# Halves of the first x tiles on two DMA queues, their scaling on three engines, and written orders at three places of a hybrid decoder block

## The chip, the cores and the metric

The kernel runs on one core of a Trainium2 chip. A core has five engines that run side by side, each with its own queue of instructions in order: TensorE (PE in the profile; PEld are its weight loads), VectorE (DVE), ScalarE (ACT), GpSimd (POOL) and SyncE (SP), which here only issues DMAs. ScalarE and GpSimd can issue DMAs too. Matrix products are written to PSUM, which has banks of 128 x 512 float32; all other tiles lie in SBUF. The metric is the device time of one execution in microseconds (us).

## The reference

The input x is 512 x 1024 float32. The block computes

```python
h = rmsnorm(x, norm1_g)
z = h @ w_in + b_in                      # split in five: glu, rx, rg, ga, gb
u = silu(layernorm(causal_conv31(glu(z_glu))))
y_a = u @ conv_w_out + conv_b_out
y_b = (rg_lru(causal_conv4(z_rx)) * gelu(z_rg)) @ lru_w_out
x = x + (sigmoid(z_ga) * y_a + sigmoid(z_gb) * y_b) @ w_mix_out
h = rmsnorm(x, norm2_g)
x = x + (silu(h @ w1) * (h @ w3)) @ w2
out = rmsnorm(x, norm_f_g)
```

where rmsnorm multiplies each row by the reciprocal root of its mean square and by a gain per column. For what follows three places matter: the first rmsnorm and the first columns of `h @ w_in`; the addition of the mixing product to x; and the last rmsnorm with the stores of the output.

## The kernel before, in words

Rows of x are taken in four tiles of 128 (t = 0 to 3), each in two halves of 512 columns: `xt[t][0]` and `xt[t][1]`. Every matrix product of float32 accuracy is made of three products of parts: each operand is split into a high part h (a copy to the type float32r) and a low part l (operand minus h), and h·h, h·l and l·h are accumulated (`mm3`, line 554). A weight chunk of 1024 columns a partition is loaded to a `raw` tile (`load_chunk`, 152), then its h is copied and its l subtracted (`emit_chunk`, 161). For the first chunk this is `first_parts` (128): VectorE copies the first 512 columns, GpSimd the second 512, and GpSimd subtracts both halves.

The start is as follows. SP issues the loads of x tiles 0 and 1, one DMA each (`load_x`, 508), two loads of parameter rows (`load_rows`, 499), the first weight chunk and the rest. ScalarE loads its table, warms a root (518) and makes a tile of ones (525). PE multiplies ones in the meantime (530). For each tile, half the sum of squares is made by VectorE in one reduction (`half_sum`, 640), the other half by ScalarE, then the root (`root`, 645 and 646) and VectorE's reciprocal. VectorE scales the halves in place (`scale_half`, 653). PE transposes the scaled rows 128 x 128 (`turn_rows`, 619) and the parameter rows (`rows_turned`, 542). ScalarE then writes the high parts of h (628), VectorE the low parts (629), and PE multiplies with the first chunk (673), in an order in which the products that need late parts come late.

The order of work on an engine comes from two sources. Most of the program is ordered by a planner, which takes the instructions in the order of the program as ranks and plays them through with estimated costs. Inside `tc.manual_schedule(engines=...)` the named engines keep the order as written. Before the change the first such region (684) names PE, ScalarE, VectorE and SP, so GpSimd is ordered by the planner there.

The mixing product and the last product are done in a scheme with seven products of quarters in place of eight (`Sevenfold.run`, 1173). At the end of its first group, products r1 and r2 of two row blocks i = 0, 1 lie in four PSUM banks, and VectorE adds each to x (`plus`, 1180). The mixing product alone is made with `behind=True`: what is split next for later products waits in VectorE's queue behind the last of these additions. The banks of r1 are accumulated into further by the second group, the banks of r2 become free for new products. After the second group VectorE makes five more additions, and the third group (`third`, 1215) accumulates into the banks of r1 again.

The last output tile is finished by `finish_last` (1587): add the last product in two halves of 256 columns, square and sum (ScalarE 1596, VectorE 1597), root and reciprocal (1598, 1600), scale with gain and reciprocal (1599, 1601, 1602, 1604), and store in three DMAs (SP 1603 and 1605, ScalarE 1606).

The core of the written order at the start:

```python
        r0 = first_sums(0)
        vec.reciprocal(r0, r0)
        scale_half(0, 0, r0)
        r1 = first_sums(1)
        scale_half(0, 1, r0)
        turn_rows(0, turned)
        vec.reciprocal(r1, r1)
        scale_half(1, 0, r1)
        rows_turned(0, n_first)
        scale_half(1, 1, r1)
        emit_to(1)
        turn_rows(1, turned)
```

Of the kernel before, what the change touches and what calls it, by code (L numbers as in the profile page):

```python
# [85 lines left out]
def tile_block(ctx, tc, a, out):  # L86
# [41 lines left out]
    def first_parts(h, l, full):  # L128
        vec.tensor_copy(h[:, :T], full[:, :T])
        pool_e.tensor_copy(h[:, T:], full[:, T:])  # L130
# [21 lines left out]
    def load_chunk(i):  # L152
        key, src, kt, cols = chunks[i][:4]
        raw = raws.tile([P, 1024], F32, tag="raw", name=f"raw_{key}")
        if callable(src):
# [343 lines left out]
    def load_rows(i):  # L499
        lo, m, src = parts[i]  # L500
        b, r = row_at(lo)
        nc.sync.dma_start(rowt[b][r : r + m, :P], src)
# [5 lines left out]
    def load_x(t):  # L508
        if t < PIECES:
# [4 lines left out]

    eps_t = consts.tile([P, 1], F32, name="eps_t")
# [15 lines left out]

    first = [i for i, (lo, _, _) in enumerate(parts) if lo < n_first]
    load_x(0)
    load_x(1)
    for i in first:
        load_rows(i)
# [77 lines left out]
    def turn_rows(t, ps):  # L614

        for c in (range(ND), (0, 3, 1, 2, 4, 7, 5, 6))[len(ps) == 6]:
# [35 lines left out]
    def scale_half(t, h, r):  # L652
        vec.tensor_scalar(out=xt[t][h], in0=xt[t][h], scalar1=r, scalar2=None, op0=ALU.mult)
# [30 lines left out]
    with tc.manual_schedule(engines={ET.PE, ET.Activation, ET.DVE, ET.SP}):  # L684
# [10 lines left out]
        rows_turned(0, n_first)  # L695
        scale_half(1, 1, r1)
# [433 lines left out]
    class Sevenfold:  # L1130
# [42 lines left out]
        def run(self, sums, begun, end):  # L1173
# [16 lines left out]
            for k in range(kh):  # L1190
# [396 lines left out]
    def finish_last(t, rest, plus_to):  # L1587
# [5 lines left out]
        for cs in HALVES:  # L1593
            plus_to(cs)
        x_ = x2[t][0]
        act.activation(junk[1][:, LO], x_[:, LO], AF.Square, accum_out=ss[:, 1:2])
        vec.tensor_tensor_reduce(out=o[0][:, HI], in0=x_[:, HI], in1=x_[:, HI], scale=1.0 / D, scalar=ss[:, 0:1], op0=ALU.mult, op1=ALU.add, accum_out=r)
        act.activation(r, ss[:, 1:2], AF.Sqrt, scale=1.0 / D, bias=r)
        vec.tensor_tensor(out=o[0][:, LO], in0=x_[:, LO], in1=gf[0][:, LO], op=ALU.mult)
        vec.reciprocal(r, r)  # L1600
        act.activation(o[1], o[1], AF.Copy, scale=r)
        vec.tensor_scalar(out=o[0][:, LO], in0=o[0][:, LO], scalar1=r, scalar2=None, op0=ALU.mult)
# [63 lines left out]
```

## Time and profile before

| what | value |
|---|---|
| median of 3 runs | 789.91 us (789.61 to 791.22) |
| profiled execution, its own time | 789.9 us |
| its span, first to last instruction | 788.1 us |
| TensorE busy | 779.7 us, 99% |
| VectorE, ScalarE, GpSimd busy | 679.0, 472.5, 363.6 us |
| moved by DMA | 199.04 MB, mean 253 GB/s |
| mean granted TensorE clock | 0.998 |

The span begins at 0; all times of rows count from there. A row of a timeline reads: start, duration, engine, line of the kernel, operation, output <- inputs, shapes, how many (x2: two merged into one row, the duration then runs from the start of the first to the end of the last). In brackets stands how long the engine had been idle and what ended that. An engine name with q (SPq, ACTq) is its sequencer, here one that issues a DMA: the duration is that of the issue, not of the transfer. Buffer numbers are left out of tile names.

### The profile page before, as it was taken

The numbers are of one execution on the slowest core, as the hardware profiler recorded it, in microseconds if no ns is written. First come the engines' busy times: TensorE is split into PE (matmuls) and PEld (weight loads), VectorE is DVE, ScalarE is ACT, GpSimd is POOL, SyncE is SP. The second block draws the span as 40 slices with busy tenths as digits, with TensorE's granted clock in tenths as the row PEclk, the third lists the DMA queues.
The fourth block names the chain that finished last, engine by engine and source line by source line (L and its number), as shares of the span: only waits on it lengthen the run. The fifth ranks groups of instructions, "written<-read, shape, count | busy, mean of one in ns | idle before, by whom it ended". The sixth has DMA issues, their size and how long they took to land.

```text
span 788.1 us, 12480 instructions
## 1 busy us (share of the span) xinstructions
PE 779.7 (99%) x4322; PEld 680.1 (86%) x4322; DVE 679.0 (86%) x1064; ACT 472.5 (60%) x693; POOL 363.6 (46%) x353
## 2 busy tenths in 40 slices
PE   9999999999999999999999999999999999999996
PEld 8988888888888888888887898999999999888885
DVE  6389998888989996999799969888777798999957
ACT  7544678966685966564325666555555555556843
POOL 3367777788779899545650591122222222000000
PEclk9999999999999999999999999999999999999999
DMA  7565989899889979999977896678998898779652
GB/s 226 144 192 156 271 237 264 246 260 296 256 239 297 269 213 272 294 284 304 321 270 250 253 287 200 200 243 306 334 307 282 297 309 302 239 238 266 204 169 107
DMA packets 191972, 199.04 MB, mean 253 GB/s; under 512 B 15245, under 2 KB 154149, under 8 KB 191909
## 3 DMA queue, kind: packets, MB, share of 16 engines
q1 hardware_dynamic: 182805, 166.52, 70.5%
q0 software_dynamic: 8960, 31.46, 11.7%
q8 instruction: 34, 0.56, 0.3%
q14 instruction: 29, 0.24, 0.1%
q10 hardware_dynamic: 144, 0.26, 0.1%
HBM read 146.30 MB, written 38.80 MB: 235 GB/s over the span
## 4 chain that ended last, share of the span: by engine, by line
PE 85%; DVE 8%; DMA 3%; issue 2%; ACT 1%; DVEq 0%; SPq 0%; ACTq 0%
PE z L563 36%; PE fr L1400 24%; PE or L1171 13%; PE f L563 3%; PE yb L563 3%; PE mxr L1171 3%; DMA raw_co<-in_conv_w_out_dram 2%; PE g L997 2%; PE fr L1444 1%; DVE hl_mxb L118 1%; DVE hl_co L118 1%; DMA raw_lo<-in_lru_w_out_dram 1%; DVE sga L1238 1%; DVE u L844 1%; PE th L603 1%
## 5 line engine op out<-in xcount | busy, mean ns | idle before, releaser
L797 DVE SCALAR_TENSOR_TENSOR cv<-u,par,cv 128x507 f32<-128x507 f32 (+15 forms) x240 | 162.6, 734 | 1.8 <-ACT cv L793 0.9
L118 POOL TENSOR_TENSOR hl_in<-raw_in,hl_in 128x1024 fp32r<-128x1024 f32 (+1 forms) x52 | 124.2, 2400 | 41.2 <-ACT hl_in L122 34.8
L118 POOL TENSOR_TENSOR fws<-fws 128x256 f32<-128x256 f32 x120 | 98.8, 825 | 80.3 <-DMA fws<-in_ffn_w_dram 74.3
L403 POOL DMA_DIRECT2D ot<-fwso x21 | 15.4, 733 | 164.1 <-DVE fwso L118 154.3
L1400 PE MATMUL fr<-hs_0h,hl_ft 128*128 128x256 f32 x320 | 59.2, 283 | 0.0
L122 ACT CAST hl_in<-raw_in 128x1024 fp32r<-128x1024 f32 x50 | 51.7, 1047 | 4.9 <-DMA raw_in<-in_w_in_dram 4.9
L118 DVE TENSOR_TENSOR hl_ft<-raw_ft,hl_ft 128x1024 fp32r<-128x1024 f32 x39 | 47.6, 1220 | 5.2 <-ACT hl_ft L122 5.2
L1400 PEld LDWEIGHTS fr<-hs_0h,hl_ft 128*128 128x128 f32 x320 | 50.6, 192 | 0.0
L122 ACT CAST hl_ft<-raw_ft 128x1024 fp32r<-128x1024 f32 x40 | 41.7, 1047 | 12.0 <-PE fr L1400 7.4
L118 DVE TENSOR_TENSOR hl_fb<-raw_fb,hl_fb 128x1024 fp32r<-128x1024 f32 x29 | 35.7, 1231 | 11.5 <-ACT hl_fb L122 11.5
L1400 PE MATMUL fr<-hs_0l,hl_ft 128*128 128x256 f32 x160 | 45.3, 283 | 0.0
L122 ACT CAST hl_fb<-raw_fb 128x1024 fp32r<-128x1024 f32 x30 | 31.5, 1049 | 18.2 <-PE fr L1400 12.2
L563 PE MATMUL z<-h10h,hl_in 128*128 128x512 f32 (+1 forms) x108 | 41.1, 382 | 0.0
L563 PE MATMUL z<-h12h,hl_in 128*128 128x512 f32 (+1 forms) x108 | 40.8, 379 | 0.0
L563 PE MATMUL z<-h14h,hl_in 128*128 128x512 f32 (+1 forms) x108 | 40.8, 379 | 0.0
L563 PE MATMUL z<-h15h,hl_in 128*128 128x512 f32 (+1 forms) x108 | 40.8, 379 | 0.0
L563 PE MATMUL z<-h16h,hl_in 128*128 128x512 f32 (+1 forms) x108 | 40.8, 379 | 0.0
L563 PE MATMUL z<-h13h,hl_in 128*128 128x512 f32 (+1 forms) x108 | 40.8, 379 | 0.0
L563 PE MATMUL z<-h11h,hl_in 128*128 128x512 f32 (+1 forms) x108 | 40.8, 379 | 0.0
L563 PE MATMUL z<-h17h,hl_in 128*128 128x512 f32 (+1 forms) x108 | 40.8, 379 | 0.0
L122 ACT CAST hl_ob<-raw_ob 128x1024 fp32r<-128x1024 f32 (+1 forms) x23 | 23.4, 1016 | 23.0 <-PE or L1171 12.3
L397 POOL TENSOR_TENSOR fws<-fws 128x256 f32<-128x256 f32 x40 | 32.5, 814 | 3.0
(930 smaller groups left out, 2596.9 us busy)
## 6 DMA issues: line engine op xcount, KB each, us to landing
raw_in<-in_w_in_dram SPq DMA_DIRECT2D x52, 512.0 KB
fws<-in_ffn_w_dram SPq DMA_DIRECT2D x40, 512.0 KB
raw_ft<-fs SPq DMA_DIRECT2D x34, 512.0 KB
fs<-fws SPq DMA_DIRECT2D x21, 512.0 KB
ot<-fwso POOLq DMA_DIRECT2D x21, 512.0 KB, 6.2
fwso<-in_ffn_w_dram POOLq DMA_DIRECT2D x40, 256.0 KB, 7.2
fs<-fws POOLq DMA_DIRECT2D x19, 512.0 KB, 4.6
raw_ob<-in_ffn_w_dram SPq DMA_DIRECT2D x33, 256.0 KB
```

What stands on the lines that cost most here:

```text
L118: return eng.tensor_tensor(out=o, in0=x, in1=y, op=ALU.subtract)
L122: copy(h, full)
L397: eng.tensor_tensor(out=q11, in0=q22, in1=q11, op=ALU.add)
L403: return queue.dma_start(dest, raw.rearrange("p (m n) -> p m n", n=256))
L563: pe.matmul(ps, l, r, start=i == 0, stop=i == n - 1)
L603: pe.transpose(ps[:, t * P : (t + 1) * P], src, ident)
L797: vec.scalar_tensor_tensor(out=acc[:, s:], in0=u[c][:, : T - s], scalar=dw(c, s), in1=acc[:, s:], op0=ALU.mult, op1=ALU.add)
L844: vec.tensor_tensor(out=u[c], in0=u[c], in1=rs, op=ALU.mult)
L997: pe.matmul(ps[:HB], head_chunk[0][:ROWS_G, g, h % 2, m, :], ext[h][m][:ROWS_G], start=m == 0, stop=m == 1)
L1171: pe.matmul(banks[i][:, cs], l_[:, ts], r_[:, cs], start=start and n == 0, stop=stop and n == 2, skip_group_check=again)
L1238: vec.scalar_tensor_tensor(out=o, in0=ps, scalar=pc("conv_b_out", j), in1=o, op0=ALU.add, op1=ALU.mult)
L1400: pe.matmul(ps[:, HALVES[i]], lw[:, c, :], rx_, start=not (again or i or c or m), stop=bool(i and c == 3 and m == 2), skip_group_check=True,)
```

## The change

- At the start the halves of x tiles 0 and 1 are loaded by two DMAs each, the first half from SP's queue and the second from ScalarE's; the two first loads of parameter rows go to ScalarE's queue as well. These loads are now issued ahead of ScalarE's table load.
- The first weight chunk is loaded in two DMAs of four blocks of rows each, that is of 512 columns of the raw tile. In `first_parts` GpSimd copies the first half, VectorE the second.
- x is scaled on three engines: the second half of tile 0 on GpSimd, the second half of tile 1 on ScalarE, the first halves on VectorE. The sums of tile 1 and the transposes of the parameter rows are written ahead of the scaling of tile 0's first half. Tile 0's second half is transposed first. GpSimd's order is as written in this region too.
- In the mixing product the four additions come in the order r1 of both row blocks, then r2 of both, behind all four products.
- In `finish_last` everything from the last additions on is in written order (ScalarE, VectorE, SP); ScalarE's last scaling is in two halves; the output's last tile goes out in four DMAs of 256 columns, three from SP and one from ScalarE.

```diff
     def first_parts(h, l, full):
-        vec.tensor_copy(h[:, :T], full[:, :T])
-        pool_e.tensor_copy(h[:, T:], full[:, T:])
+        pool_e.tensor_copy(h[:, :T], full[:, :T])
+        vec.tensor_copy(h[:, T:], full[:, T:])
         for cs in (slice(0, T), slice(T, 2 * T)):
             newest["sub"] = sub(pool_e, l[:, cs], full[:, cs], h[:, cs].bitcast(F32)).ins
...
-        if callable(src):
+        if i == 0:
+            for k in range(0, kt, 4):
+                nc.sync.dma_start(raw[:, k * cols : (k + 4) * cols].rearrange("p (k n) -> p k n", k=4), src[:, k : k + 4, :])
+        elif callable(src):
...
     def load_x(t):
+        if t < 2:
+            for h, queue in enumerate((nc.sync, nc.scalar)):
+                queue.dma_start(xt[t][h], x_nat[:, t, h * T : (h + 1) * T])
+            return
...
+    first = [i for i, (lo, _, _) in enumerate(parts) if lo < n_first]
+    load_x(0)
+    load_x(1)
+    for i in first:
+        load_rows(i, nc.scalar)
     eps_t = consts.tile([P, 1], F32, name="eps_t")
...
+        some = (0, 3, 1, 2, 4, 7, 5, 6)
+        for c in (range(ND), some[4:] + some[:4] if t == 0 else some)[len(ps) == 6]:
...
-    with tc.manual_schedule(engines={ET.PE, ET.Activation, ET.DVE, ET.SP}):
+    with tc.manual_schedule(engines={ET.PE, ET.Activation, ET.DVE, ET.SP, ET.Pool}):
...
         r0 = first_sums(0)
         vec.reciprocal(r0, r0)
+        scale_half(0, 1, r0, pool_e)
+        r1 = first_sums(1)
+        rows_turned(0, n_first)
         scale_half(0, 0, r0)
-        r1 = first_sums(1)
-        scale_half(0, 1, r0)
         turn_rows(0, turned)
         vec.reciprocal(r1, r1)
         scale_half(1, 0, r1)
-        rows_turned(0, n_first)
-        scale_half(1, 1, r1)
+        scale_half(1, 1, r1, act)
...
-                    if ends and r == 1:
+                    if ends and r == 1 and not self.behind:
                         plus(i, 0, r1[i])
-                        last_sum = plus(i, 0, r2[i]).ins
+                        plus(i, 0, r2[i])
+                    if ends and (r, i) == (1, 1) and self.behind:
+                        for b_ in (r1, r2):
+                            for t in range(2):
+                                last_sum = plus(t, 0, b_[t]).ins
...
+        with tc.manual_schedule(engines={ET.Activation, ET.DVE, ET.SP}):
+            for cs in HALVES:
+                plus_to(cs)
...
+            for cs in HALVES:
+                act.activation(o[1][:, cs], o[1][:, cs], AF.Copy, scale=r)
+            vec.tensor_scalar(out=o[0][:, LO], in0=o[0][:, LO], scalar1=r, scalar2=None, op0=ALU.mult)
+            vec.scalar_tensor_tensor(out=o[0][:, HI], in0=x_[:, HI], scalar=r, in1=gf[0][:, HI], op0=ALU.mult, op1=ALU.mult)
+            for queue, i, cs in ((nc.sync, 0, LO), (nc.sync, 1, LO), (nc.scalar, 1, HI), (nc.sync, 0, HI)):
+                queue.dma_start(o_nat[:, t, i * T + cs.start : i * T + cs.stop], o[i][:, cs])
```

More of the change, by code (lines that the diff above doesn't have):

```diff
@@ L530, in tile_block @@
         pe.matmul(wp[:, :P], ones, ones, start=True, stop=True)
[L532 to L536, printed above, removed]
     def rows_turned(c0, c1):
@@ L650, in first_sums, with scale_half @@
         return root(t, half_sum(t))
-    def scale_half(t, h, r):
-        vec.tensor_scalar(out=xt[t][h], in0=xt[t][h], scalar1=r, scalar2=None, op0=ALU.mult)
+    def scale_half(t, h, r, eng=vec):
+        if eng is act:
+            act.activation(xt[t][h], xt[t][h], AF.Copy, scale=r)
+        else:
+            eng.tensor_scalar(out=xt[t][h], in0=xt[t][h], scalar1=r, scalar2=None, op0=ALU.mult)
     HALVES = [slice(0, 256), slice(256, 512)]
```

23 lines of the change are left out of this document (7 added, 16 removed).

## The prediction

> **What bounds the kernel now.** First I read the busy table of the page, then the stages by window.
>
> ```profile
> PE 779.7 (99%) x4322; PEld 680.1 (86%) x4322; DVE 679.0 (86%) x1064; ACT 472.5 (60%) x693; POOL 363.6 (46%) x353
> ```
>
> ```profile
> 350.00:400.00 50.00, 50.00 (x222) 41.40 (x221) 43.27 (x56) 19.11 (x26) 27.07 (x28) 1.00 1.02 320
> 400.00:441.00 41.00, 40.63 (x179) 33.25 (x178) 40.26 (x61) 21.05 (x31) 5.85 (x8) 1.00 0.81 257
> ```
>
> TensorE (columns: length, then busy time of PE, PEld, DVE, ACT, POOL, then clock and DMA) is busy nearly without a break. So an edit can win time only where PE waits: at the start, before the first weights and inputs are ready; once near 428.9 us; and in the tail, after the last matmul. The change touches exactly these three. The second row also says that VectorE is busy for 40.26 of 41 us around the middle place, which decides the second term. The profiled execution took 789.9 us (span 788.1), the median of the runs 789.91, so no correction is needed.
>
> **Start: the present path.** Three views of the first 10 us, by engine: VectorE, ScalarE, TensorE.
>
> ```profile
> 5.78 0.49 DVE L653 TENSOR_SCALAR x<-x,stats 128x512 f32<-128x512 f32 x1
> 6.18 0.68 DVE L640 CUSTOM_DVE_ANT_0 n1j<-x 128x512 f32<-128x512 f32 x1
> ...
> 7.49 0.88 DVE L653 TENSOR_SCALAR x<-x,stats 128x512 f32<-128x512 f32 x2
> 8.29 0.42 DVE L129 CAST hl_in<-raw_in 128x512 fp32r<-128x512 f32 x1
> 9.16 0.48 DVE L629 SCALAR_TENSOR_TENSOR h10l<-tx,par,h10h 128x256 fp32r<-128x256 f32 x1 [0.45 <-ACT h10h L628]
> ```
>
> ```profile
> 0.73 1.28 ACT L518 ACT_TABLE_LOAD   x1 [0.73 <-PEq L1652]
> 2.03 0.20 ACT L518 ACTIVATE warm<-eps_t 128x1 f32<-128x1 f32 x1
> 2.14 0.28 ACT L525 CAST onesr<-ones 128x128 fp32r<-128x128 f32 x1
> 4.45 0.63 ACT L645 ACTIVATE n1j<-x 128x512 f32<-128x512 f32 x1 [2.03 <-DMA x<-in_x_dram]
> ...
> 5.75 0.63 ACT L645 ACTIVATE n1j<-x 128x512 f32<-128x512 f32 x1 [0.20 <-DMA x<-in_x_dram]
> ```
>
> ```profile
> 7.92 0.27 PE L542 MATMUL par_ps<-ident,rows 60*128 60x60 f32 x1
> 8.12 1.09 PE L619 MATMUL tx<-ident,x 128*128 128x128 f32 x8
> ```
>
> Tile 0 of x lands at about 4.45, tile 1 at 5.75. VectorE has to scale tile 0 (0.49 a half), reduce half of tile 1 (0.68) and scale tile 1 (two in 0.88); the first half of tile 1 is ready at 7.98, the transposes follow at 8.12 behind the parameter rows, and the low parts of h begin on VectorE at 9.16.
>
> **Start: the issue moves.** The two halves of tiles 0 and 1 and the two row loads put four DMA issues at the head of ScalarE's queue. An issue there costs 0.40 us, and one on SP at the same moment 0.38:
>
> ```profile
> 784.57 0.40 ACTq L1606 DMA_DIRECT2D out_dram<-of  x1
> ```
>
> ```profile
> 784.63 0.38 SPq L1605 DMA_DIRECT2D out_dram<-of  x1
> ```
>
> So 4 x 0.40 = 1.6 us push ScalarE's table load, its warm activation and the cast that ends at 2.42 to about 4.0. The cover is the 2.03 us in which ScalarE waits for x; 0.4 us of it is left. If x came 0.4 us earlier, the cover would be gone. I price this at nothing, and the landing of x at nothing too: the same bytes go ahead of the same first weights. Bounds for x: 0.3 earlier (nearest: SP needs one 0.38 issue less before tile 1 and the weights), 0.4 later (ScalarE's share waits for one of SP's issues). I take 0, as nothing else lies ahead of x on either queue. SP's later loads stand behind one issue fewer (two rows gone, one weight half and no x issue more).
>
> The Trainium skill, "DMA: Bandwidth & Descriptors", section "Issuing engines are not separate DMA queues", says that transfers from several engines share the same 16 DMA engines, so a second queue saves only issue time. By it the landing of x does not move at all; no row here shows two queues loading at once, so it is only in line with my zero.
>
> **Start: scaling on three engines.** If nothing collided: the reduction of tile 1 no longer stands behind a 0.49 us scale, r1 comes about 0.3 earlier, the second half of tile 1 goes to ScalarE, and the parameter transpose leaves the path; the first low part of h would come 0.45 earlier (the best bound). But VectorE and GpSimd block each other. Views: the timeline at 129 us (one row of each engine) and at 459 us.
>
> ```profile
> 129.37 2.41 POOL L118 TENSOR_TENSOR hl_in<-raw_in,hl_in 128x1024 fp32r<-128x1024 f32 x1 [1.02 <-ACT hl_in L122]
> ```
>
> ```profile
> 129.46 2.86 DVE L891 SCALAR_TENSOR_TENSOR xb<-th,xb 128x512 f32<-128x512 f32 x1
> ```
>
> ```profile
> 459.20 0.80 POOL L118 TENSOR_TENSOR fwso<-fwso 128x256 f32<-128x256 f32 x1
> ...
> 459.51 0.77 DVE L1280 TENSOR_SCALAR xs<-x,stats 128x512 f32<-128x512 f32 x1
> ```
>
> The VectorE operation with two SBUF inputs ends at 132.32, 0.54 after GpSimd's at 131.78. The scale of 128x512, 0.49 alone (row at 5.78), takes 0.77 and ends at 460.28, 0.28 after GpSimd's end at 460.00. So VectorE stood still until GpSimd was done. And GpSimd waits too:
>
> ```profile
> 8.27 0.91 POOL L130 CAST hl_in<-raw_in 128x512 fp32r<-128x512 f32 x1 [6.83 <-DMA raw_in<-in_w_in_dram]
> 9.15 2.54 POOL L118 TENSOR_TENSOR hl_in<-raw_in,hl_in 128x512 fp32r<-128x512 f32 x2
> ```
>
> Its cast ends at 9.18, 0.47 after VectorE's cast (8.71). I read 0.47 as the cost of a one-input GpSimd operation once the other is done, and 0.47 to 0.91 as its bounds; the new scale on GpSimd has the same shape. Step by step, with 0.47:
> - r0 is ready at 5.75. VectorE's reduction and GpSimd's scale start within 0.1 of each other; I let VectorE win: reduction to about 6.46, GpSimd's scale to 6.95, VectorE's scale of the other half to 6.95 + 0.28 = 7.23, r1 by 7.4.
> - The first weight chunk now comes as two DMAs. x1 lands at 5.75, the whole chunk at 8.27; halfway, 7.0, is my estimate for its first half. GpSimd casts it from 7.23 (behind VectorE's scale) to 7.70; VectorE's scale of tile 1 waits for that and ends at 7.98, as before.
> - GpSimd then subtracts (half of 2.54, so 1.27), behind that scale: 7.98 to about 9.13 (1.15, as part of it overlaps the wait).
> - VectorE's cast of the second weight half can begin at 8.29, but stands behind that subtraction: 9.13 + 0.28 = 9.41. It is ahead of the low parts of h in the written order, so these begin at about 9.43 and not at 9.16: 0.27 late.
>
> What of that PE feels, by the end of the chain of low parts against their use:
>
> ```profile
> 11.91 0.48 DVE L629 SCALAR_TENSOR_TENSOR h17l<-tx,par,h17h 128x256 fp32r<-128x256 f32 x1
> ...
> 12.60 0.28 PE L673 MATMUL z<-h17l,hl_in 128*128 128x256 f32 x1
> ```
>
> Ready 12.39, used 12.60: 0.2 of slack, less in the middle of the chain. Of 0.27 about 0.15 arrives. Start: **+0.15**, bounds -0.45 (no collision) and +0.5 (GpSimd wins the first race, and the first weight half comes later than 7.0, so that the subtraction ends still later).
>
> The Trainium skill, "SBUF — State Buffer", section "Who interferes with whom", says the same against this change: a VectorE operation with two SBUF inputs, or in a two-port mode such as a scale, and a GpSimd operation that reads SBUF take one shared port pair, and the second to start blocks until the first is done. The rows at 129 and 459 us agree (2.86 and 0.77 against 0.68 and 0.49). By the rule the start loses 0.15, without it it gains 0.45.
>
> **Middle: the four additions.** VectorE and PE around the one stall, and what follows.
>
> ```profile
> 426.76 2.87 DVE L1120 TENSOR_TENSOR x<-mxr,x 128x512 f32<-128x512 f32 x4
> ...
> 441.30 0.15 DVE L580 TENSOR_SCALAR stats<-stats 128x1 f32<-128x1 f32 x1 [0.46 <-ACT xs L579]
> 441.38 3.28 DVE L1120 TENSOR_TENSOR x<-mxr,x 128x512 f32<-128x512 f32 x5
> ```
>
> ```profile
> 428.89 0.50 PE L1171 MATMUL mxr<-hl_mxt,mxvb0h 128*128 128x512 f32 x1 [0.37 <-DVE x L1120]
> ```
>
> ```profile
> 444.72 0.50 PE L1171 MATMUL mxr<-mxt40h,mxvb0h 128*128 128x512 f32 x1
> ```
>
> PE waits at 428.89 for the third of the four additions (r1 of the second row block). The edit makes that one the second, 0.7 earlier (2.87 / 4). PE idled 0.37 by its row, some 0.6 by the spacing of matmul starts, since ends are modelled; I take it that 0.6 goes. But what is late next is the third group of products at 444.72, which cannot accumulate before the five additions that end at 444.66. These stand behind a ScalarE statistic (441.30), and VectorE has 0.74 us of idle time in 41: no work is taken from it. PE would reach that point 0.6 earlier and wait there for 0.6. **0**, bounds -0.6 (the planner lets the five additions begin earlier) and +0.1.
>
> **Tail.** VectorE, then ScalarE after the last addition.
>
> ```profile
> 782.38 0.42 DVE L1599 TENSOR_TENSOR of<-x2b,gfh 128x256 f32<-128x256 f32 x1
> 782.71 0.48 DVE L1597 CUSTOM_DVE_ANT_0 of<-x2b,stats 128x256 f32<-128x256 f32 x1
> ...
> 783.62 0.16 DVE L1600 RECIPROCAL stats<-stats 128x1 f32<-128x1 f32 x1 [0.42 <-ACT stats L1598]
> ```
>
> ```profile
> 783.82 0.72 ACT L1601 ACTIVATE of<-of,stats 128x512 f32<-128x512 f32 x1 [0.23 <-DVE stats L1600]
> ```
>
> As written, the reduction (L1597) comes ahead of the product (L1599), which moves under ScalarE's root: 782.71 - 782.38 = 0.33 off the path to the reciprocal. Then ScalarE's 0.72 scale is halved, and four stores of 128 KB replace two of 128 and one of 256. SP now issues three, one after another: 0.38 + 0.38 + 0.38 after its first at about 783.88 (the reciprocal's 783.78 less 0.33, a half-width scale, a hand-over) put the third's end at 785.02, where the last issue of before ended (784.63 + 0.38 = 785.01). So the 0.33 does not reach the last issue; the gain is that only 128 KB, not 384, is issued in the last 0.4 us, and that the bytes start 0.33 earlier. At some 290 GB/s (the mean rate of the row for 400 to 441 is 257, that of 350 to 400 is 320), the 256 KB fewer are worth up to 0.9, but the stores are then bound by their own start, 0.33 earlier, so the gain is between 0.33 and 0.65; bound on the other side 0 (the third issue decides all). **-0.45**.
>
> **Sum.** +0.15 + 0 - 0.45 = -0.3: 789.9 - 0.3 = **789.6 us**.
>
> **Rivals.**
> - *Nothing collides and the middle pays* (for: starts within 0.1 of each other may fall well, the weight half may come early; against: the two blocked rows, the full VectorE): -0.45 - 0.6 - 0.45 = -1.5, 788.4 us.
> - *The other side: the issues of the two queues go one at a time.* Four from SP and four from ScalarE, 8 x 0.40 from 0.73 on, end at 3.9; the table load and what follows it take as long as now (0.73 to 2.42, 1.7), so the first square starts at 5.6 and not at 4.45: +1.15 at the start. It decides as soon as ScalarE's four issues take over 2.0 us. Against it: the two rows at 784.6, which overlap by 0.34 and are no longer for it. 789.6 + 1.15 = 790.8 us. The Trainium skill, "Perfetto Trace Analysis", section "DMA Instruction — HWDGE (DVE, Sync)", speaks for it: the descriptor generator is locked by one issue at a time. The trace, with 0.40 and 0.38 side by side, does not agree.
> - *The planner orders something else.* Work outside the written regions is ordered by the planner, whose picture of the start and of the four additions changes. Where VectorE has 0.74 us to spare in 41, one conversion of GpSimd's length (2.41) set ahead of a needed one makes PE wait that long: 789.6 + 2.4 = 792.0. It decides once an operation slips by more than that slack. Against: at 350 to 400 VectorE has 6.7 idle of 50, and PE none.
>
> **How the numbers follow.** Forecast 0.53, no collision 0.20, issues one at a time 0.12, planner 0.15. About 0.2%, 1.58 us, is what can be told from no change: 788.33 to 791.49. Faster: half of the second case and a little of the first, 0.13; slower: most of the planner's case and a part of the third, 0.18; within: 0.69. The sum of all lower bounds is 789.9 - 0.45 - 0.6 - 0.65 = 788.2, and 788.1 with x a little earlier; the upper bounds give 790.4, the third case 790.8, and up to 791.6 part of the fourth. The forecast's own range is 788.9 to 790.4.
>
> **What would show it.** Start: GpSimd's scale of x ending after 6.8, VectorE's weight cast (L129's twin) stretched over 0.8 us with its end 0.28 after a GpSimd subtraction, first low part of h between 9.2 and 9.7; ScalarE's cast of ones done before the first square. Middle: no wait at 428.9, and a wait of about 0.6 before the first product of the third group near 444. Tail: reduction straight behind the last addition, reciprocal 0.3 earlier against that addition, last store issued at about the same distance from it. Wrong if the low parts begin before 9.0, if the middle wait does not come back, if ScalarE's four issues take 2 us or more, or if PE shows a new wait between 24 and 428 us.

## The result, and the profile after

The changed kernel takes 793.18 us (median of 22 runs) against 791.13 for the kernel before in 22 runs beside it: ratio 1.0027, 95% interval 1.0014 to 1.0040. It is slower by 2.05 us, and the forecast, 0.3 us faster (789.6, its own range 788.9 to 790.4), had the wrong sign. Only the prediction's planner case (792.0) lay as far up, and that did not occur. (The three runs on which the forecast was built, with a median of 789.91, lay low in the spread of the kernel before.) The profiled executions took 793.2 us (span 791.4) and 789.9 us (span 788.1). To place the 3.3 us between them I compared the starts of TensorE's matched products in the two traces: 1.59 us are lost before 17 us, nothing more up to 405 us, 1.51 between 405 and 450, nothing up to the tail, 0.2 behind the last product. Since the middle differs from execution to execution (below), the start is the first place to look at.

The start of the changed kernel, from the timeline by engine (start, length, engine, line, operation, and in brackets the idle time and what ended it). ScalarE and its queue, then SP's queue:

```profile
0.74 0.91 ACTq L515 DMA_DIRECT2D x<-in_x_dram  x2
...
2.29 0.32 ACTq L505 DMA_DIRECT2D rows<-in_b_in_dram  x1
...
4.04 0.28 ACT L538 CAST onesr<-ones 128x128 fp32r<-128x128 f32 x1
4.23 0.63 ACT L654 ACTIVATE n1j<-x 128x512 f32<-128x512 f32 x1
...
7.37 0.73 ACT L663 ACTIVATE x<-x,stats 128x512 f32<-128x512 f32 x1
```

```profile
0.74 0.89 SPq L515 DMA_DIRECT2D x<-in_x_dram  x2
```

The two queues issue side by side. ScalarE's four issues end at 2.61 (1.87 us, where 1.6 was forecast), its cast runs from 4.04 to 4.32, and the first square follows the cast at 4.23 without a wait. In this execution the cover is just used up, and nothing is lost. So far the prediction holds. GpSimd and VectorE:

```profile
5.80 2.07 POOL L665 TENSOR_SCALAR x<-x,stats 128x512 f32<-128x512 f32 x1 [4.36 <-DVE stats L700]
7.84 0.78 POOL L129 CAST hl_in<-raw_in 128x512 fp32r<-128x512 f32 x1
```

```profile
5.82 0.69 DVE L649 CUSTOM_DVE_ANT_0 n1j<-x 128x512 f32<-128x512 f32 x1
...
6.45 0.82 DVE L665 TENSOR_SCALAR x<-x,stats 128x512 f32<-128x512 f32 x1
...
7.37 0.78 DVE L665 TENSOR_SCALAR x<-x,stats 128x512 f32<-128x512 f32 x1
8.07 0.82 DVE L130 CAST hl_in<-raw_in 128x512 fp32r<-128x512 f32 x1
10.71 0.48 DVE L638 SCALAR_TENSOR_TENSOR h10l<-tx,par,h10h 128x256 fp32r<-128x256 f32 x1 [1.82 <-ACT h10h L637]
```

The last scale of tile 0 in the kernel before:

```profile
6.79 0.48 DVE L653 TENSOR_SCALAR x<-x,stats 128x512 f32<-128x512 f32 x1
```

GpSimd's scale of half a tile takes 2.07 us and ends at 7.87, where before all of tile 0 was scaled by 7.27. The collisions are there (0.82 and 0.78 in place of 0.49), but only the second is as the prediction has it, ending 0.28 after GpSimd's scale (8.15); the first ends at 7.27, 0.60 ahead of GpSimd's end. The low part of h is late for another reason: VectorE is idle for 1.82 us ahead of it and waits for the transposes. TensorE:

```profile
1.09 4.69 PE L543 MATMUL warm<-ones 128*128 128x128 f32 x24 [1.09 <-DVE ones L536]
6.98 0.24 PE L550 MATMUL par_ps<-ident,rows 60*128 60x60 f32 x1 [1.21 <-DMA rows<-in_b_in_dram]
7.92 3.46 PE L628 MATMUL tx<-ident,x 128*128 128x128 f32 x16 [0.70 <-POOL x L665]
11.04 0.56 PE L685 MATMUL z<-h10h,hl_in 128*128 128x256 f32 x1
```

And the first product before:

```profile
9.18 0.38 PE L673 MATMUL z<-h10h,hl_in 128*128 128x256 f32 x1
```

TensorE first waits for the parameter rows, which now stand first in its order, then for GpSimd's half of tile 0; and then sixteen transposes take 3.46 us, where eight took 1.09 before. The first product starts at 11.04, not at 9.18. The busy time by window (the window, its length, then PE, PEld, DVE, ACT, POOL, then TensorE's granted clock, the DMA share and GB/s) says why the transposes are slow:

```profile
4.83:8.24 3.41, 1.50 (x13) 1.21 (x12) 2.82 (x9) 2.26 (x8) 2.44 (x2) 0.99 1.10 312
8.24:11.65 3.41, 3.41 (x19) 3.41 (x17) 1.59 (x4) 1.45 (x5) 2.93 (x3) 0.51 1.05 352
```

From 8.24 to 11.65 the granted clock is half. In the 3.41 us before that TensorE was busy for 1.50.

The middle (VectorE's four additions, TensorE's two waits beside them):

```profile
430.31 2.88 DVE L1132 TENSOR_TENSOR x<-mxr,x 128x512 f32<-128x512 f32 x4
```

```profile
431.14 0.70 PE L1183 MATMUL mxr<-hl_mxt,mxvb0h 128*128 128x512 f32 x2 [1.24 <-DVE x L1132]
...
432.44 0.73 PE L1183 MATMUL mxr<-hl_mxt,mxvb0h 128*128 128x512 f32 x2 [0.36 <-DVE x L1132]
```

The wait that the edit was to remove is still there (0.36 at 432.44; before 0.37 at 428.89), with a longer one ahead of it. The tail:

```profile
784.81 0.75 DVE L1132 TENSOR_TENSOR x2b<-or,x2b 128x256 f32<-128x256 f32 x2
785.60 0.48 DVE L1614 CUSTOM_DVE_ANT_0 of<-x2b,stats 128x256 f32<-128x256 f32 x1
...
786.51 0.17 DVE L1617 RECIPROCAL stats<-stats 128x1 f32<-128x1 f32 x1
```

```profile
787.09 1.30 SPq L1623 DMA_DIRECT2D out_dram<-of  x3
```

The last additions before:

```profile
781.72 0.75 DVE L1120 TENSOR_TENSOR x2b<-or,x2b 128x256 f32<-128x256 f32 x2
```

The reciprocal starts 1.70 after the start of the last additions (1.90 before), but SP's third issue ends at 788.39, 3.58 after them (3.29 before).

### The profile page after: what moved, and what is told of

Read it like the earlier page. It is cut to its first block, busy times and chain, and to the rows that moved or that the text cites. A ratio compares the mean times of both kernels' runs of the same rounds, so it can differ in the third digit from the quotient of the medians.

```text
span 791.4 us, 12490 instructions
## 1 busy us (share of the span) xinstructions
PE 780.0 (99%) x4322; PEld 680.8 (86%) x4322; DVE 682.6 (86%) x1062; ACT 473.3 (60%) x695; POOL 364.5 (46%) x354
## 4 chain that ended last, share of the span: by engine, by line
PE 53%; DVE 12%; DMA 12%; POOL 9%; issue 5%; SPq 4%; ACT 3%; POOLq 0%; DVEq 0%; ACTq 0%
PE fr L1416 24%; PE or L1183 13%; PE z L571 8%; POOL hl_in L118 4%; DMA raw_in<-in_w_in_dram 4%; POOL fws L118 3%; PE f L571 3%; PE mxr L1183 3%; DMA fws<-in_ffn_w_dram 2%; DMA mxws<-in_w_mix_out_dram 2%; SPq L994 2%; DMA fs<-fws 2%; DMA raw_co<-in_conv_w_out_dram 2%; DVE hl_lo L118 1%; DVE cv L809 1%
## 5 line engine op out<-in xcount | busy, mean ns | idle before, releaser
L122 ACT CAST hl_fb<-raw_fb 128x1024 fp32r<-128x1024 f32 x30 | 31.5, 1050 | 18.4 <-PE fr L1416 10.4
```

The source lines that it names most:

```text
L122: copy(h, full)
```

## The experiments

Theory A: the start loses by TensorE's idle time, which lowers its clock. Theory B: the data are late, by GpSimd's scale and the rows, whatever the clock. Theory C: the middle's 1.5 us is not the edit's.

**GpSimd's scale by itself.** Three GpSimd operations are added to the kernel before, near its beginning, where VectorE has nothing to do.

```
+    pool_e.memset(heads_b[:, P:], 1.0)
+    pool_e.tensor_scalar(out=rowt[0][:, P:], in0=heads_b[:, P:], scalar1=eps_t, ...mult)
+    pool_e.tensor_scalar(out=rowt[0][:, P:], in0=heads_b[:, P:], scalar1=2.0, ...mult)
```

> The kernel before with three GpSimd operations added at 1.5 us, where GpSimd and VectorE have nothing to do: a fill of 128x384, a scale of 128x384 by a column (the form of the added scale) and the same scale by a constant. Nobody reads the results. If GpSimd's scale is slow by itself, the scale by a column takes about 1.5 us (0.75 of 2.07). If it was slow because VectorE held it up, it takes about 0.35 to 0.7 us (0.75 of 0.47 to 0.91, the bounds of the prediction). The rest of the kernel should stay as it is.

```profile
1.75 1.25 POOL L523 TENSOR_SCALAR rows<-rowsh,eps_t 128x384 f32<-128x384 f32 x1
9.12 0.86 POOL L130 CAST hl_in<-raw_in 128x512 fp32r<-128x512 f32 x1 [6.12 <-DMA raw_in<-in_w_in_dram]
9.97 1.16 POOL L524 TENSOR_SCALAR rows<-rowsh 128x384 f32<-128x384 f32 x1
```

With VectorE idle (from 1.0 to 4.8 us) the scale of 384 columns takes 1.25 us, which makes 1.67 for 512 if it grows with the columns. It is slow by itself; a cast of 512 takes 0.78 to 0.86. The rest did not stay as it was: the scale by a constant was put behind the cast, and the first low weights came so late that TensorE waited for them for 1.2 us. One run took 792.16. The Trainium skill, "GPSIMD Engine Reference", section "3.1 Elementwise — side-by-side cycle accounting", gives 769 ns for 512 elements as the best case of a tight loop. The cast agrees (0.78); the scale by a column takes about twice that (1.67 by the estimate, 1.57 to 2.10 in the traces of the changed start).

**TensorE kept busy by a longer warm-up.** `WARM = 12` becomes 21 in the changed kernel.

> The changed kernel with 21 warm-up products in place of 12, so that TensorE has work until about 7.8 us (the nine more take about 0.22 us each after the warm-up's present end at 5.78). Nothing else is changed; the warm-up stands ahead of all else in TensorE's order. Theory A (the start is lost because TensorE idles from 5.78 to 7.92 but for one operation, and its granted clock is then 0.50 until 11.6): the clock stays at 1.00 from 8 to 12 us, the sixteen transposes take about 2 us and not 3.46, the first product z<-h10h starts at 9.5 to 9.9 and not at 11.04, and the span comes down by 1.1 to 1.5 us. Theory B (the data are late, behind GpSimd's scale and the rows on ScalarE's queue; the clock is a symptom that costs nothing): the clock may stay up, but the first product starts at 10.7 or later and the span comes down by under 0.4 us.

The clock stayed at 1.00 and the transposes took 1.97 us. But the warm-up lasted to 8.53, the rows' transposition and with it ScalarE's scale came behind it, and the first product started at 10.68. Ratio to before 1.0013 (0.9996 to 1.0030). The clock's part of A is shown, the gain not, for I made the warm-up too long.

**The gap filled in two places.**

```
-WARM = 12
+WARM = 16
...
         rows_turned(0, n_first)
+        for _ in range(3):
+            pe.matmul(wp[:, :P], ones, ones, start=True, stop=True)
```

> The changed kernel with 16 warm-up products in place of 12 and three more between the transposition of the parameter rows and that of tile 0, so that TensorE has something to do in most of the time from 5.8 to 7.9 us and nothing has to wait for it for more than about 0.3 us. Theory A: clock 1.00 throughout, the transposes in about 2.0 us, starting at 7.9 to 8.2; first product at 9.9 to 10.4; what is left against before (9.18) is the late data, 0.7 to 1.2. Theory B: first product at 10.7 or later.

Clock 1.00, transposes 1.97 us, first product at 10.49 (a little over A's 10.4; GpSimd's scale ended at 8.41 here, as x came 0.5 later than in the changed kernel's trace). One run of 793.55. So with the clock up the first product is still about 1 us late against the first square (5.75 us behind it, 4.73 before): A and B are both true, side by side.

**The scale back on VectorE; the rows back on SP.** Two edits of the changed kernel, each alone: `scale_half(0, 1, r0)` without `pool_e`, and `load_rows(i)` without `nc.scalar`.

> The changed kernel with the first scale (second half of tile 0) back on VectorE, ahead of the reduction of tile 1; the queues, the written orders and ScalarE's scale stay as changed. If GpSimd's scale of 2.07 us is what holds the transposes (tile 0's are released by it at 7.87): tile 0 is scaled by 6.9, the transposes of it begin at 7.2 (behind the parameter rows' transposition at 6.98), TensorE idles under 1.5 us in one piece, the clock stays at 1.00 and the first product starts at 9.2 to 9.6. If the rows' landing at 6.85 on ScalarE's queue is enough to lower the clock by itself, the clock is 0.50 all the same and the first product starts at 10.3 or later.

> The changed kernel with the two row loads issued by SP, ahead of the first weights, in place of ScalarE. If the queue is what makes the rows late (6.85 as changed, 5.88 before), they land near 5.9 and the parameter rows are transposed at about 6.0, right behind the warm-up; the tile 0 transposes still wait for GpSimd's scale until about 7.9, so that TensorE idles 1.6 us in one piece. Theory A in its strict form (any idle stretch of over 1 us at this place lowers the clock) expects the clock at 0.50 from about 8.2 on and the first product near 11.0; before the change TensorE idled about 0.7 in one piece at the most and kept its clock. If a short piece of work in the middle resets the count, the clock could stay up and the first product start near 9.7.

The scale on VectorE, GpSimd's and VectorE's rows:

```profile
7.81 1.32 POOL L118 TENSOR_TENSOR hl_in<-raw_in,hl_in 128x512 fp32r<-128x512 f32 x1
```

```profile
8.11 1.30 DVE L665 TENSOR_SCALAR x<-x,stats 128x512 f32<-128x512 f32 x1
```

The rows on SP, TensorE:

```profile
6.50 0.36 PE L550 MATMUL par_ps<-ident,rows 60*128 60x60 f32 x1
8.23 1.97 PE L628 MATMUL tx<-ident,x 128*128 128x128 f32 x16 [1.37 <-POOL x L665]
10.26 0.36 PE L685 MATMUL z<-h10h,hl_in 128*128 128x256 f32 x1
```

Neither did what was hoped (one run each, of 797.86 and of 791.17). With the scale on VectorE the first product starts at 10.62: GpSimd, free of it and with the first weight half in at 6.9, subtracts at 7.81 and holds up VectorE's scale of tile 1 (0.49 becomes 1.30). With the rows on SP they are there before the warm-up ends, but GpSimd's scale keeps tile 0 until 8.18. And TensorE's 1.37 us in one piece did not lower the clock: A in its strict form is false.

**Scale and weight split undone, the rows left on ScalarE's queue.** Beside `pool_e`, the two loads of the first weight chunk become one again.

> The changed kernel with two things undone at the start: the second half of tile 0 is scaled on VectorE (ahead of the reduction of tile 1), and the first weight chunk comes as one load again, so that GpSimd has nothing to do before about 8.2 us. The two queues, ScalarE's scale and the written orders stay. Measured against the start of ScalarE's first square (4.45 before, first product 4.73 later; 5.4 to 5.8 later in the variants with GpSimd's scale and the clock at 1.00, 5.96 with the scale on VectorE and the split load). If GpSimd's early work is the whole of the late data: first product 4.6 to 4.9 after the first square. Rival (the rows' queue or TensorE's written order cost it): 5.3 or more.

```profile
8.12 0.24 PE L547 MATMUL par_ps<-ident,rows 60*128 60x60 f32 x1 [1.53 <-DMA rows<-in_b_in_dram]
```

First product at 10.31, 5.47 after the first square: the rival's number (one run, of 791.27). All of tile 0 is scaled at 7.84, but the rows land at 8.1, and TensorE's order has them first. Why they land as late as 6.9 to 8.1 is not shown; before, they are issued on SP's queue ahead of the first weights, here beside them on another queue.

**All three undone.** As the last, and the rows on SP.

> The changed kernel with three things undone at the start: the second half of tile 0 is scaled on VectorE, the first weight chunk comes as one load, and SP issues the parameter rows ahead of the weights. What stays of the start: x on two queues, ScalarE's scale of the last half, the written orders. With one of the three undone the first product came 5.5 to 6.0 us after ScalarE's first square (4.73 before; rows on SP alone 5.65, scale on VectorE alone 5.96, scale and split undone 5.47, there behind rows that landed at 8.1). Theory (each of three late things covers the others: GpSimd's scale, GpSimd's early weight work that blocks VectorE's scale of tile 1, the rows on ScalarE's queue): with all three gone the first product comes 4.4 to 4.8 us after the first square, and TensorE runs -0.2 to +0.3 us against before from 20 us on. Rival (TensorE's written order, rows ahead of tile 0 and tile 0's second half first, costs it): 5.1 or more. The time by the theory: before's, within 0.5 us.

First product 9.57, first square 4.58: 4.99 later, between the theory's 4.8 and the rival's 5.1, with 0.17 of it because the second half of tile 0 lands that much later on ScalarE's queue. Ratio to before 1.0002 (0.9983 to 1.0020), median 791.27 against 791.39. By the last column of the table below (23.90, where before has 23.66 and the changed kernel with its clock up 24.30) the three together are 0.40 of the 0.64 us of late data; 0.24 is left. Undoing one or two of them gained nothing there (24.50 to 24.85), which fits that each was covered by the others.

**The clock in further executions of the changed kernel.** First the start alone on the kernel before, then three more executions of the changed kernel itself, called a, b and c, one run each (791.87, 794.88 and 790.55).

> The kernel before with the part of the change that lies at the start alone (two queues, split first weight chunk, three engines, written orders); middle and tail as before. If the start carries the loss: slower by 1.0 to 1.6 us (ratio 1.0013 to 1.0020). Theory A in its strict form (TensorE's idle time after the warm-up always lowers the clock): clock 0.50 from about 8.2 us on, sixteen transposes in about 3.5 us, first product near 11.0. Its looser form (the data are late by about 1.0, and the clock falls in some executions only, on top): where the clock stays at 1.00, the transposes take 2.0 us and the first product starts at 10.2 to 10.4, as with the rows on SP. Rival (the loss is in the middle or the tail): within 0.3 us of before.

> The changed kernel itself, a second look at its start. Window theory: the clock is granted by spans of about 3.4 us whose phase differs from execution to execution; the warm-up's products go from 0.21 to 0.11 us apart at the end of one such span, and the clock falls at the end of the next if TensorE was busy in it for less than about half (1.50 of 3.41 us where it fell, 1.84 and more where it held). So the later the warm-up's products speed up, the more of the next span is filled by transposes: speeding up before about 4.9 us lets the clock fall or come close to it, after about 5.2 it holds. Where it holds, the transposition of the last parameter rows (25.07 in the changed kernel's trace, 23.5 to 24.0 in kernels with the start of before) starts at 24.2 to 24.7; where it falls, at 25.0 to 25.4. Rival (the clock falls in every execution of this kernel): 0.50 from about 8 to 11 us again, wherever the speeding up lies.

> The changed kernel itself, a third look, with the expectations of the second: by the window theory the clock falls only where the warm-up's products speed up before about 4.9 us, and the last parameter rows are transposed at 24.2 to 24.7 where it holds, at 25.0 to 25.4 where it falls; by the rival it falls again.

> The changed kernel itself, a fourth look, with the expectations of the second. With the two others it says how much of the loss at the start is there in every execution (the late data, 0.6 to 1.0 us) and how much in some only (the clock, about 0.8).

The start alone, GpSimd's row and the windows:

```profile
5.99 1.57 POOL L665 TENSOR_SCALAR x<-x,stats 128x512 f32<-128x512 f32 x1 [4.55 <-DVE stats L700]
```

```profile
4.83:8.24 3.41, 1.84 (x16) 1.54 (x15) 2.69 (x8) 2.14 (x8) 2.25 (x2) 1.00 1.10 320
8.24:11.65 3.41, 3.35 (x22) 2.48 (x21) 3.41 (x7) 2.86 (x8) 2.66 (x3) 1.00 1.06 368
```

Execution b, windows:

```profile
4.42:7.83 3.41, 1.46 (x13) 1.17 (x11) 2.81 (x8) 2.51 (x8) 2.12 (x2) 1.00 1.10 330
7.83:11.24 3.41, 3.41 (x17) 3.41 (x18) 1.34 (x4) 1.26 (x4) 3.19 (x3) 0.50 1.07 354
```

| kernel | warm-up speeds up at | PE busy in the next 3.41 us | clock then | last parameter rows transposed |
|---|---|---|---|---|
| changed, first trace | 4.83 | 1.50 | 0.51 | 25.07 |
| start alone | 4.85 | 1.84 | 1.00 | 24.24 |
| changed, execution a | 5.94 | 1.96 | 1.00 | 24.29 |
| changed, execution b | 4.42 | 1.46 | 0.50 | 25.13 |
| changed, execution c | 5.73 | 1.82 | 1.00 | 24.36 |

(The second column is where the starts of the warm-up's products go from 0.21 to 0.11 us apart; the last is the start of the transposition of `rowsh`.) The clock fell in the two executions in which TensorE was busy for 1.46 and 1.50 of the 3.41 us that follow the speeding up, and held from 1.82 on. It does not fall in every execution: the rival is out. A threshold is not shown. Counted in the same way in other places, the clock fell after 1.80 us busy of 3.41 (long warm-up, from 429.58 on) and held after 1.78 (execution b, from 188.71 on).

Four traces with the start of before have 23.48, 23.55, 23.64 and 23.97 in the last column, 23.66 on the mean. So the late data cost 24.30 - 23.66 = 0.64 us (three traces), the fallen clock 25.10 - 24.30 = 0.80 more in two of five. In these two x came some 0.3 us earlier (first square at 4.23 and 4.36, in the others at 4.43 to 4.74); counted from the first square the fall costs 1.1. (The start alone has its first product at 9.79, earlier than the 10.2 expected. Here GpSimd's scale took only 1.57, and VectorE's reduction was stretched, to 1.06.) The start alone measured 1.0028 (1.0012 to 1.0044), as much as the whole change.

The Trainium skill, "TensorE: Matmul & The Clock Gate", section "Part 1: The HAM clock gate", has the window free-running, 3413 ns long, with a phase that differs by run. The traces agree: in the first the clock is up from 4.78 to 8.19 and at half from there to 11.61, twice 3.41 us, and in the five traces it first comes up at 4.39 to 5.97.

How often it falls can also be read from the mean granted clock, which is on record for every run. One fall of 3.41 us to half lowers the mean over 791 us by 0.0022. (A stretch at half clock behind the last product is in the mean of every kernel.)

| kernel | runs | mean granted clock | lowest |
|---|---|---|---|
| before, four sets of runs | 86 | 0.9979 to 0.9983 | 0.996 |
| changed | 22 | 0.9962 | 0.992 |
| start alone | 12 | 0.9964 | 0.993 |
| changed, long warm-up | 12 | 0.9979 | 0.996 |
| changed, all three undone | 12 | 0.9980 | 0.996 |

Six of the 22 runs of the changed kernel are at 0.992 to 0.995, where no run of before is; their median is 796.0 us, that of the other 16 is 792.7. On the mean the changed kernel has 0.0020 less than before (0.9982 over all 86 runs), that is some 0.9 falls more per execution and not the 0.4 of five traces. A fall costs 0.80 us as measured at the start, and up to 1.7 where TensorE has work throughout (half of 3.41), so this is worth 0.7 to 1.5 us, an estimate. Where in the execution the further falls lie is not recorded. With the long warm-up, or with all three undone, they are gone.

**Middle and tail alone, and the additions forced.** The second kernel adds, to the edit of the first, that each addition is issued after the last:

```
+                                with tc.issue_after(last_sum) if last_sum else nullcontext():
                                     last_sum = plus(t, 0, b_[t]).ins
```

> The kernel before with the two other parts alone: the four additions written in the other order, and the tail. Theory C (what the traces show between 400 and 450 us is a spread that every kernel has, the edit there does nothing): 0.4 us faster to 0.2 us slower than before (ratio 0.9995 to 1.0003), the four additions in VectorE's old order (first bank of block 0, second bank of block 0, then block 1), the wait ahead of the second group of products with mxvb0h at 0.5 to 0.6 us. Rival (the edit in the middle costs): slower by 0.5 us or more. The tail alone, by the prediction, 0.45 faster; by the one trace of the changed kernel 0 to 0.2.

> As the kernel with middle and tail alone, but each of the four additions is told to be issued after the one before it, so that the written order (first banks of both blocks, then second banks) is the one that VectorE gets. By the prediction's step: the wait ahead of the second group of products with mxvb0h (0.57 us by the distance of the starts) is gone or much shorter, and a wait of about that size stands ahead of the third group's first product some 15 us later; the time is that of middle and tail alone within 0.3 us. Rival (what is won stays won): 0.5 to 0.6 us faster than that kernel (ratio lower by about 0.0007).

Without force VectorE's order does not change at all: first bank, second bank of block 0, then of block 1, as before, presumably because the planner sets it by when each sum is ready. Compared instruction by instruction, with their waits, the kernel with middle and tail alone is the kernel before up to the last 6 us. Yet its trace waits for 1.94 us near 430 where the trace of before waits for 0.54, and it measured 1.0019 (1.0001 to 1.0036), more than was expected and with an interval above 1. That is what the same work spreads: in the traces these two waits come to 0.2 to 2.0 us. C holds for the edit; and a comparison of this size can be off by some 1.5 us.

Forced, the additions run in the written order, and TensorE:

```profile
429.87 0.70 PE L1171 MATMUL mxr<-hl_mxt,mxvb0h 128*128 128x512 f32 x2 [0.38 <-DVE x L1120]
430.40 0.39 PE L1171 MATMUL mxr<-hl_mxt,mxvb0l 128*128 128x512 f32 x1
430.63 0.61 PE L1171 MATMUL mxr<-hl_mxt,mxvb0h 128*128 128x512 f32 x2
```

```profile
447.06 0.51 PE L1171 MATMUL mxr<-mxt40h,mxvb0h 128*128 128x512 f32 x1 [0.33 <-DVE x L1120]
```

The second group starts 0.76 us after the first (1.30 in the traces where it waits), and a wait of 0.50 by the spacing of starts stands at 447.06, in the third group. In this one trace the 0.54 looks moved, not won; but executions a and b, with the old order, have waits of 0.25 and 0.48 between 446 and 450 as well, so this is not shown. The time, 0.9995 (0.9975 to 1.0014), is in line with that and can't settle it by itself.

**Two attempts to win.** The first takes the kernel before with the new middle and tail, and reorders its start with GpSimd left alone:

```
         r0 = first_sums(0)
         vec.reciprocal(r0, r0)
+        r1 = first_sums(1)
         scale_half(0, 0, r0)
+        vec.reciprocal(r1, r1)
         scale_half(0, 1, r0)
...
+        scale_half(1, 1, r1, act)
```

> The kernel before with its loads unchanged, and at the start only this: VectorE reduces tile 1 before it scales tile 0, and ScalarE scales the second half of tile 1; GpSimd is left alone. Middle and tail as in the change. If the collisions with GpSimd are what made the change lose: tile 1 is scaled 0.4 to 0.7 earlier against the first square, the first product comes 4.2 to 4.5 after it (4.73 before), TensorE is 0.2 to 0.5 ahead from 20 us on. Rival: the low parts of the first weights, which GpSimd makes from 8.2 on as before, are waited for, and less than 0.1 is left. The time: 0.2 to 0.6 under before, inside what the runs spread.

Tile 1 was scaled 0.5 earlier, but the first half of tile 0 came 0.6 later, and TensorE needs 2 us for the sixteen transposes, which it could begin only at 6.97 (6.37 before): first product 4.99 after the first square, no gain. Ratio 1.0013 (0.9993 to 1.0033).

The second takes a conversion from VectorE in its full stretch, tied to the first addition by a copy of one column:

```
-                h, l = split_to(...)
+                if key == "mxb22_2":
+                    act.copy(h, rv)
+                    put_off.append((l, rv, h))
...
                         plus(i, 0, r1[i])
+                        if put_off:
+                            tiny = pool_e.tensor_copy(ones[:, :1], sums[i][0][:, :1]).ins
+                            with tc.issue_after(tiny):
+                                newest["sub"] = sub(pool_e, l, rv, h.bitcast(F32)).ins
```

> The kernel before with one conversion (the low part of the mixer's weight chunk b22 of k = 2, 1.22 us on VectorE just ahead of the four additions) given to GpSimd, tied to the first of the four additions by a copy of one column, so that it runs (some 2.4 us) while VectorE adds, with one operand of each addition in PSUM. GpSimd has nothing to do from 420 to 441 us. If additions with an operand in PSUM are not blocked by GpSimd: the four additions still take 2.9 us, VectorE's backlog shrinks by 1.1, the two waits of TensorE near 430 (0.54 to 1.94 in sum in the runs so far) shrink by as much, as far as they reach, and the median falls by 0.5 to 1.1 us. Rival: GpSimd blocks VectorE there too: the additions or the conversion behind them are 1 us or more longer, and the time does not fall.

```profile
429.64 2.38 POOL L119 TENSOR_TENSOR hl_mxb<-raw_mxb,hl_mxb 128x1024 fp32r<-128x1024 f32 x1
```

```profile
428.74 0.68 DVE L1126 TENSOR_TENSOR x<-mxr,x 128x512 f32<-128x512 f32 x1
429.71 2.31 DVE L1126 TENSOR_TENSOR x<-mxr,x 128x512 f32<-128x512 f32 x3 [0.29 <-POOL ones L1207]
```

The three additions beside GpSimd's 2.38 us are no longer than before (2.31, and 2.87 for four): with one operand in PSUM they were not held up. But the tie itself held the second addition for 0.29, and further on TensorE waited for 0.67, 0.50 and 1.59 us between 446 and 454, after which its clock was at half for 3.4 us. Slower: 1.0034 (1.0015 to 1.0053). The likely cause, that the raw weight buffer comes free 5 us later, was not tried.

## Why the prediction was wrong

*Start, +0.15 forecast, +0.64 measured with the clock up, and more where it falls.* The failed step is the price of GpSimd's scale: "I read 0.47 as the cost of a one-input GpSimd operation once the other is done, and 0.47 to 0.91 as its bounds". It came from the remainder of a cast that ran beside VectorE's, another operation; the scale takes about 1.7 by itself (estimated from 1.25 for three quarters of it) and 1.57 to 2.10 beside VectorE. With it fell what hung on it: tile 0 is ready at 7.87, and TensorE's new order asks for just that half first. That this price alone costs the 0.64 is not shown, as the start was no faster with only that scale undone. The second wrong step is that "the parameter transpose leaves the path": it went ahead of tile 0's, and the rows on ScalarE's queue came later (6.85 to 8.1). The third thing was not in the working at all, a term put at nothing without a word: with both waits behind the warm-up TensorE's clock can fall to half. The path that the prediction followed (low parts at 9.43, held by VectorE's weight cast) never bound: the cast ended at 8.89, and the low parts waited for the transposes.

What was right: the four issues on ScalarE are hidden (1.87 us, under the 2 that were to decide), x lands where it did (within 0.3), issues of two queues don't exclude each other (that rival is out), VectorE's scales and weight cast are stretched to about 0.8 beside GpSimd.

*Middle, 0 forecast.* Right in size, wrong in its first step: "the edit makes that one the second" never happened, the edit changed no instruction. The reason given for 0 agrees with the one trace in which the order is forced, no more. The planner's rival (2.4 us later) did not occur: the order outside the written places is the same.

*Tail, -0.45 forecast.* The reciprocal comes 0.20 earlier, not 0.33: the reduction needs the second addition's result and starts 0.79 after the additions' start (785.60 - 784.81), where the product that stood ahead of it could start after 0.66 (782.38 - 781.72). SP's three issues end 0.29 later than the two of before, not at the same distance: the third waits for its turn. From the start of TensorE's last product to the end of the span it is 6.8 us with the old tail (three traces) and 6.7 with the new (three traces), both with the start of before, so the step is worth 0.1 to 0.2. In the changed kernel it is 7.0 (7.1 with the changed start and the old tail), some 0.2 more than before and not 0.45 less; the last section says why.

*The sum* of what the traces and clocks show is 0.64 for the late data, 0.7 to 1.5 for the falls of the clock and 0.2 for the end: 1.5 to 2.3 us. The measured 2.05 lies in it, and its interval (1.1 to 3.2 us) holds all of it. It is an estimate. The waits of the middle, which spread by as much in a kernel with an unchanged program, and those near 190 us (0.3 to 1.8 us in some traces of either kind) may have a part in the 2.05, and how large it is stays open.

## What to carry to other kernels

Price an operation that moves to another engine by a row of that operation on that engine, or measure it alone first; the leftover of another operation is no price. When a short stage is shifted, add up TensorE's waits over some 3.4 us, the length of its clock's steps here, and do not look for a single long gap. And where a planner sets the order, see that an edit has changed the instructions before asking what it is worth.

## What was not expected of the hardware

- The clock gate acts in the middle too. In the trace with the long warm-up TensorE waits for 1.93 us near 431, and the clock then falls for 3.4 us; the row for one of these (windows):

```profile
434.00:435.00 1.00, 1.00 (x4) 0.72 (x3) 1.00 (x2) 0.00 (x0) 0.00 (x0) 0.50 1.11 358
```

  So a wait of 2 us can cost another 1.7 (half of 3.4), in some executions: the traces of the changed kernel and of middle and tail alone have the same wait there and no fall. The three traces with such a fall in the middle are the three longest (796.08, 796.84 and 797.86), so it is one source of the spread of single times (789.6 to 794.6 before, 791.1 to 799.8 after).
- The end of this program depends on the number of the semaphore (the counter that tells of a landing) that the last store has. SP waits for the DMA semaphores one behind the other, some 0.06 us each. Before, the last landing raises number 108, and two waits follow the one for it; in the changed kernel, whose loads at the start are other in number, it raises 102, and six follow. The span then ends 1.26 us after the last landing (791.4 - 790.14), not 1.0 (788.1 - 787.09).
- VectorE's reduction with both inputs from one SBUF tile ran in 0.69 (row at 5.82) beside GpSimd's scale that had started 0.02 earlier. In the trace with the start alone, where GpSimd's took 1.57, it took 1.06. So which of the two is held up is not the same in every execution.
